# A hybrid block on one core: the interleaved part planned by a model of the engines, with TensorE tied to the plan

## The chip, the cores and the metric

One NeuronCore of one Trainium2 chip runs the whole kernel. The metric is the device time of one execution, in microseconds (us). The kernel before takes 1144.53 us, the median of 3 runs (1142.67 to 1146.72).

## The reference

A transformer block in fp32 for one sequence of 512 positions with 1024 channels. Three mixers of width 512 with 8 heads of 64 read one input projection: softmax attention with a forget gate ("fox"), a gated linear recurrence in chunks of 64 ("hgrn") and a delta-rule recurrence ("rwkv"). Their outputs go through a projection each, are gated and summed, and a convolutional feed-forward part follows.

```python
mod = silu(c) @ w_ada + b_ada                       # shifts, scales and gates, 6 x 1024
h = rms_norm(x) * norm1_g * (1 + sc1) + sh1
fox_p, hgrn_p, rwkv_p, gate_p = split(h @ w_in)     # 1024 -> 1544 + 2048 + 1792 + 3072
y_fox = fox_attention(...)      # rms norm of q and k per head, softmax per 128 queries
y_hgrn = hgrn2_branch(...)      # chunked recurrence, rms norm per head, gate
y_rwkv = rwkv7_branch(...)      # low-rank decay and rate, k normed per head, recurrence, group norm
merged = sum(sigmoid(g_i) * (y_i @ w_branch[i]) for i in range(3))
x = x + gt1 * (merged @ w_out)
h = rms_norm(x) * norm2_g * (1 + sc2) + sh2
u = causal_dwconv(h @ w_up, conv_w, conv_b)         # 5632 channels, 3 taps
x = x + gt2 * ((u_a * silu(u_b)) @ w_down)
```

## The kernel before

Every large product is made of three products of operands that are rounded to the fp32r type and their remainders (`mm3`: high times high, high times low, low times high), with 128x128 weights and 512 moving columns. A weight block comes by SP's queue (`raw`), ScalarE makes its high part (`whi`), VectorE or GpSimd the low one (`wlo`). These are called big products here; they write `mm` tiles in PSUM. All other products are plain fp32, write `br` tiles, and many use a part of the array only: 64x64 (chunks of the recurrences), 128x64, 64x128, 128x32 or 32x32.

The program has a start (modulation, first norm, first projection columns), an interleaved part, and an end (`w_out`, second norm, `w_up`, `w_down`). The interleaved part is the one that changes. It consists of Python generators, the streams: `rwkv_b`, `rwkv_a`, `hgrn` and `fox` for four pairs of heads each (`gi` from 0 to 3), `prep`, `ada_stream` (the later modulation columns, on VectorE), and `big`, which walks the list of projection, gate and merge jobs. `run` (L111) asks them in turn to emit their next piece of code. A stream gives back a latency by hand (`yield 2.0`), and is asked again when a clock `clk` has passed it; `clk` is a count of TensorE's time by rough prices in `mm` (L81) and `transpose` (L91). The first stream in the list whose time has come is taken, so the big products fill what the others leave. `need` (L97) makes a stream wait for what another has posted with a latency.

What `run` emits is then put in order once more by the framework's scheduler, engine by engine, which may draw a ready instruction ahead of an earlier one, TensorE's included. After that each engine executes its own order.

`head_sums` (L447) sums squares over the 64 channels of a head: four products on quarters of the array (a 128x32 weight, 128 moving columns), a VectorE copy `hs` (L457), and a transpose by TensorE. Callers are `rwkv_a` (`ksq`), `hgrn` (`pr`), `fox` (two tiles, `qsq`) and `ada_stream` (`adac`): 16 calls with 20 tiles. In `rwkv_a` the low-rank products of `a` and the decay use a 128-row high part and a 64-row low part of the weight (`w2h`, `w2l`).

Chains that the prediction speaks of, with their lines: softmax of `fox` (logits, masked maximum L708, `nmx` L711, exponential L717, 1/sum L722, scaling of `L` L723, transposes by L93, `PT`); norms of heads (`rn` or `qkr`, power on GpSimd, `rnx` L439, transposes); the state chain of `rwkv_b` (six steps of two 64x64 products and one VectorE step, `ST`, L1031) and its group norm (`gsum`, `gxc` L1051, `gvar`, `gxc` L1060, transposes); the inverse in `rwkv_a` (15 VectorE steps on `lt` and `X`, a write to DRAM `d` and a read back as `Xc`, then 32x32 products on `XZ`).

```python
            for q in range(4):
                mm(ps[32 * q:32 * q + 32, i * P:(i + 1) * P], ones[:, 0:32] if sums else K("hind32"), sq[:, q * P:(q + 1) * P])
        t = T2("hs")
        v.tensor_copy(t[:, :n], ps[:, :n])
        yield 0.6
        ps = PSB()
        for i in range(len(sqs)):
            transpose(ps[:, i * P:(i + 1) * P], t[:, i * P:(i + 1) * P], ident)
```

Of the kernel before, what the change touches and what calls it, by code (L numbers as in the profile page):

```python
# [22 lines left out]
              ("hind32", 32), ("half16", 2), ("nhalf32", 2), ("id64", 64), ("sel8", 8), ("i16", 256), ("causal", 512)]  # L23
# [17 lines left out]

@with_exitstack
def block_kernel(ctx: ExitStack, tc: tile.TileContext, I, out, dbg=None, upto=99):
    nc = tc.nc
    sync, v, s, g, pe = nc.sync, nc.vector, nc.scalar, nc.gpsimd, nc.tensor
    P = 128
# [17 lines left out]
    LAT = (0.9, 1.65)  # L64
# [15 lines left out]
    clk = [0.0]  # L80

    def mm(o, lhsT, rhs, start=True, stop=True):
        n = rhs.free_size() if hasattr(rhs, "free_size") else math.prod(rhs.shape[1:])
        if rhs.dtype == F32R:
            clk[0] += n / 2400
        else:
            half = (0.5 if lhsT.shape[0] <= 64 else 1.0) * (0.25 if math.prod(lhsT.shape[1:]) <= 32 else 1.0)
            clk[0] += half * max(0.17, n / 600)
        return pe.matmul(o, lhsT=lhsT, rhs=rhs, start=start, stop=stop)  # L89

    def transpose(o, i, idn):  # L91
        clk[0] += 0.11 if i.shape[0] > 64 else 0.07
        pe.transpose(o, i, idn)  # L93
# [3 lines left out]
    def need(*keys):  # L97
        for k in keys:
            while k not in avail:
                yield None  # L100
        t = max(avail[k][0] for k in keys) - clk[0]
        if t > 0:
            yield t
        return [avail[k][1] for k in keys]

    def post(key, val, lat=0.0):
        avail[key] = (clk[0] + lat, val)

    def run(streams):

        live = [[gen, 0.0, False] for gen in streams]  # L111
        while live:
            done = False
            for st in live:
                if st[1] > clk[0] + 1e-9:
                    continue
                c0, n0 = clk[0], len(avail)
                try:
                    lat = next(st[0])
                except StopIteration:  # L120
                    live.remove(st)
                    done = True
                    break
                if lat is None and c0 == clk[0] and n0 == len(avail):
                    continue
                lat = lat or 0.0
                st[1] = clk[0] + (lat * LAT[0] + LAT[1] if lat else 0.0)
                done = True
                break
            if not done:  # L130
                later = [st[1] for st in live if st[1] > clk[0] + 1e-9]
                assert later, "streams wait for each other"
                clk[0] = min(later)

    def PSM():
        return psm.tile([P, 512], F32, tag="mm", name=nm("mm"))

    def PSB():
        return psb.tile([P, 512], F32, tag="br", name=nm("br"))
# [186 lines left out]
    def split(raw, shape, leng):  # L326
        hi = wp.tile(list(shape), F32R, tag="whi", bufs=WB[1], name=nm("whi"))
        lo = wp.tile(list(shape), F32R, tag="wlo", bufs=WB[2], name=nm("wlo"))
# [5 lines left out]
    def load(src, r0, nr, c0, ncol):  # L334
        nld[0] += 1
        sh = [P, nr // P, ncol]
        raw = wp.tile(sh, F32, tag="raw", bufs=WB[0], name=nm("raw"))
# [111 lines left out]
    def head_sums(sqs, sums=None):  # L449

        n = len(sqs) * P
        ps = PSB()
        for i, sq in enumerate(sqs):
            for q in range(4):
                mm(ps[32 * q:32 * q + 32, i * P:(i + 1) * P], ones[:, 0:32] if sums else K("hind32"), sq[:, q * P:(q + 1) * P])
        t = T2("hs")
        v.tensor_copy(t[:, :n], ps[:, :n])  # L457
        yield 0.6
        ps = PSB()
        for i in range(len(sqs)):  # L460
# [962 lines left out]
```

## Time and profile before

| | |
|---|---|
| median of 3 runs | 1144.53 us (1142.67 to 1146.72) |
| profiled execution | 1147.7 us, its span 1145.9 us |
| TensorE (PE) busy | 1081.7 us, 94% of the span |
| VectorE (DVE) | 679.2 us, 59% |
| ScalarE (ACT) | 522.9 us, 46% |
| GpSimd (POOL) | 280.0 us, 24% |
| interleaved part | 54.5 to 719.7 us; from 613.4 us on it has big products alone |

The span is the time from the first instruction to the last in the profiled execution, and the rest of its own time lies around it. PE is TensorE's matrix products, PEld its weight loads, which overlap them. A plain fp32 product stands in the trace as two records, one for each pass; a transpose and an fp32r product as one. Matrix products are pipelined, so the start of one to the start of the next is its price, not its listed duration. The granted clock is 1.0 at 2.4 GHz and 0.5 at 1.2 GHz.

### The profile page before, as it was taken

Reading aid. Unit: us, or ns where it says so; the run is one execution under the profiler, and the core shown is the slowest. Engines: PE = TensorE matmul, PEld = TensorE weight load, DVE = VectorE, ACT = ScalarE, POOL = GpSimd, SP = SyncE. Lnnn points to the kernel's source line nnn. Section 1 sums busy time; section 2 is a strip of 40 time slices with the busy share of each in tenths; the row PEclk is TensorE's granted clock in tenths of the full one; section 3 lists DMA queues with packets and bytes.
Section 4 is the critical chain, followed back from the end, with each engine's and each line's share of the span. In section 5 each row is a group of like instructions: output and inputs, shape, how many; then the busy total and the mean of one; then the engine's idle time right before and its main releaser. Section 6 shows DMA issues by size and latency. Waiting matters only on the chain. (4 is left out here: it accounts for less than half of the span.)

```text
span 1145.9 us, 19809 instructions
## 1 busy us (share of the span) xinstructions
PE 1081.7 (94%) x7617; PEld 863.8 (75%) x7617; DVE 679.2 (59%) x1369; ACT 522.9 (46%) x965; POOL 280.0 (24%) x274
## 2 busy tenths in 40 slices
PE   4988999799999999979999999899999999999998
PEld 2566776587777777767878887678888888888886
DVE  1567665858578685784745636536666666661114
ACT  2575464255656656367434335224444444442220
POOL 4015321513334331431021613332111101101100
PEclk8999998889999999989999999899999999999999
DMA  9732233132322440334343565201333333333232
GB/s 315 206 83 71 72 101 89 37 105 72 87 95 50 125 107 20 93 89 135 85 129 102 159 201 179 85 1 56 98 99 93 101 98 96 94 100 100 93 101 83
DMA packets 175476, 117.63 MB, mean 103 GB/s; under 512 B 25360, under 2 KB 151350, under 8 KB 175382
## 3 DMA queue, kind: packets, MB, share of 16 engines
q1 hardware_dynamic: 173696, 116.22, 34.9%
q8 instruction: 60, 0.98, 0.4%
q10 hardware_dynamic: 1238, 0.12, 0.1%
q14 instruction: 34, 0.28, 0.1%
q0 software_dynamic: 448, 0.03, 0.0%
HBM read 112.57 MB, written 3.77 MB: 102 GB/s over the span
## 5 line engine op out<-in xcount | busy, mean ns | idle before, releaser
L330 ACT ACTIVATE whi<-raw 128x512 fp32r<-128x512 f32 x282 | 176.5, 629 | 355.0 <-PE mm L89 226.7
L331 DVE TENSOR_TENSOR wlo<-raw,whi 128x512 fp32r<-128x512 f32 x212 | 150.9, 714 | 156.1 <-ACT whi L330 152.7
L331 POOL TENSOR_TENSOR wlo<-raw,whi 128x512 fp32r<-128x512 f32 x70 | 97.8, 1397 | 495.3 <-ACT whi L330 475.4
L89 PE MATMUL mm<-hhi,whi 128*128 128x512 f32 x504 | 205.5, 408 | 2.6 <-ACT gt L1091 2.3
L89 PE MATMUL mm<-hhi,wlo 128*128 128x512 f32 x504 | 200.2, 397 | 0.0
L89 PE MATMUL mm<-hlo,whi 128*128 128x512 f32 x504 | 200.2, 397 | 0.0
L89 PE MATMUL mm<-h2hlo,whi 128*128 128x512 f32 (+1 forms) x376 | 141.5, 377 | 1.2 <-POOL h2hlo L1273 1.2
L89 PE MATMUL mm<-h2hhi,whi 128*128 128x512 f32 (+1 forms) x376 | 141.3, 376 | 0.0
L89 PE MATMUL mm<-h2hhi,wlo 128*128 128x512 f32 (+1 forms) x376 | 141.2, 376 | 0.0
L89 PEld LDWEIGHTS mm<-hhi,whi 128*128 128x128 f32 x504 | 95.9, 190 | 25.2 <-ACT gt L1091 2.7
L89 PEld LDWEIGHTS mm<-hhi,wlo 128*128 128x128 f32 x504 | 96.0, 190 | 20.7 <-issue 0.2
L89 PEld LDWEIGHTS mm<-hlo,whi 128*128 128x128 f32 x504 | 96.2, 191 | 18.4 <-issue 0.6
L89 PEld LDWEIGHTS mm<-h2hlo,whi 128*128 128x128 f32 x376 | 70.7, 188 | 14.9 <-POOL h2hlo L1273 2.0
L89 PEld LDWEIGHTS mm<-h2hhi,whi 128*128 128x128 f32 x376 | 70.7, 188 | 12.9
L89 PEld LDWEIGHTS mm<-h2hhi,wlo 128*128 128x128 f32 x376 | 70.7, 188 | 12.6
L1331 DVE SCALAR_TENSOR_TENSOR u<-mm,cw,u 128x511 f32<-128x511 f32 x44 | 32.9, 747 | 54.7 <-ACT u L1330 54.7
L1162 DVE SCALAR_TENSOR_TENSOR adac<-ada,cs,adac 128x512 f32<-128x512 f32 x56 | 46.0, 822 | 0.7
L89 PE MATMUL br<-wlo,ahi 128*128 128x512 f32 x110 | 42.8, 389 | 0.0
L89 PE MATMUL br<-whi,ahi 128*128 128x512 f32 x110 | 42.8, 389 | 0.0
L89 PE MATMUL br<-whi,alo 128*128 128x512 f32 x110 | 42.8, 389 | 0.0
L89 PE MATMUL mm<-yhi,whi 128*128 128x512 f32 x96 | 38.3, 399 | 0.8 <-DVE gt L1142 0.7
L89 PE MATMUL mm<-ylo,whi 128*128 128x512 f32 x96 | 37.5, 391 | 0.0
(387 smaller groups left out, 1947.5 us busy)
## 6 DMA issues: line engine op xcount, KB each, us to landing
raw<-in_w_in_dram SPq DMA_DIRECT2D x126, 256.0 KB, 3.1
ada<-in_w_ada_dram SPq DMA_DIRECT2D x96, 256.0 KB, 4.9
raw<-in_w_up_dram SPq DMA_DIRECT2D x88, 256.0 KB, 3.0
raw<-in_w_down_dram SPq DMA_DIRECT2D x44, 256.0 KB, 2.6
raw<-in_w_branch_dram SPq DMA_DIRECT2D x24, 256.0 KB, 2.7
wo<-in_w_out_dram SPq DMA_DIRECT2D x16, 256.0 KB, 4.8
x<-in_x_dram SPq DMA_DIRECT2D x8, 256.0 KB, 4.8
mg<-in_x_dram SPq DMA_DIRECT2D x8, 256.0 KB
```

Of the source, the lines that this page charges most:

```text
L89: return pe.matmul(o, lhsT=lhsT, rhs=rhs, start=start, stop=stop)
L330: s.activation(hi, raw, AF.Copy)
L331: (g if leng == "g" else v).tensor_tensor(out=lo, in0=raw, in1=hi.bitcast(F32), op=ALU.subtract)
L1162: v.scalar_tensor_tensor(out=acc, in0=raws[k], scalar=cs[:, k:k + 1], in1=acc, op0=ALU.mult, op1=ALU.add)
L1331: v.scalar_tensor_tensor(out=u[:, 1:], in0=ps[:, :511], scalar=cw[:, 1, jj:jj + 1], in1=u[:, 1:], op0=ALU.mult, op1=ALU.add)
```

## The change

The planner's clock is replaced by a class `Plan` that follows, for each tile, when it is ready and when it was last used; for each engine of VectorE, ScalarE and GpSimd, a list of busy intervals in which a new instruction takes the first gap; SP's queue and the transfers; TensorE with its array mode; and the buffers of the pools. Wrappers (`Planned`) around the engines feed it with each instruction that the code emits. A stream gives back a kind in place of a latency: "f" (free, any time it is ready), "s" (small, on a part of the array) or "b" (a big product, ready when its weight is). `run` takes a ready free stream first, holds small ones back for up to 3 us while big products are ready and the whole array is in use, and gives them all in a row then. Every product and transpose of the interleaved part is tied behind the one emitted before it, so that the scheduler leaves TensorE's order as planned; the other engines' orders are still the scheduler's. `head_sums` takes the squares as 128x128 weights and two columns (or one) as the moving operand, without a copy and a transpose. The low part of the low-rank weights is filled with zeros to 128 rows, so that its products use the whole array. In `rwkv_a` and `ada_stream` a split and the products that read it become two steps.

```diff
+SEM, DRAIN, CHANGE, ENTER = 0.08, 0.2, 0.11, 0.1
+START, HOLD, SLACK = 47.0, 3.0, 0.1
...
+    def other(self, engine, op, outs, ins):
+        n = outs[0].free_size()
...
+        if engine == "ACT":
+            took = 0.2 + 0.85e-3 * n + (0.19 if len(outs) > 1 else 0.0)
+        elif engine == "POOL":
+            took = 0.3 + 2.2e-3 * n if n > 16 else 0.2 + 0.18 * n
+        else:
+            one = len([a for a in ins if a.free_size() > 8]) < 2 and not psum
+            took = 0.17 + (0.6e-3 if one else 1.15e-3) * n + (0.08 if psum else 0.0)
+        end = self.place(engine, max(self.when((*outs, *ins)), self.slot.get(outs[0].tensor.name, 0.0)) + SEM, took)
...
+    def transfer(self, o, i):
...
+        self.sp = max(self.sp, self.when((o, i)), self.slot.get(o.tensor.name, 0.0)) + 0.1
+        self.dma = max(self.sp, self.dma) + 4 * n / 250e3
+        self.done([o], [i], self.dma + 2.0)
...
+    def in_order(emit):
+
+        if pe_last[0] is None or not strict[0]:
+            r = emit()
+        else:
+            with tc.issue_after(pe_last[0]):
+                r = emit()
+        pe_last[0] = r.ins
+        return r
...
+            small = [st for st in ready if st["kind"] == "s"]
+            free = [st for st in ready if st["kind"] == "f" and not st["big"]]
+            big = [st for st in ready if st["big"]]
+            if plan.whole() and big and small and t - left < HOLD and t - min(st["at"] for st in small) < HOLD:
+                small = []
+            pick = free or small or big
...
-    def head_sums(sqs, sums=None):
-
-        n = len(sqs) * P
-        ps = PSB()
+    def head_sums(sqs, w):
+
+        ps = PSB()
+        n = w.free_size()
         for i, sq in enumerate(sqs):
             for q in range(4):
-                mm(ps[32 * q:32 * q + 32, i * P:(i + 1) * P], ones[:, 0:32] if sums else K("hind32"), sq[:, q * P:(q + 1) * P])
-        t = T2("hs")
-        v.tensor_copy(t[:, :n], ps[:, :n])
-        yield 0.6
...
+                o = (i * 4 + q) * n
+                mm(ps[:, o:o + n], sq[:, q * P:(q + 1) * P], w)
...
-            mm(ps, w2s[i][1][:, gs], L1[i][0:64, :], False, True)
+            mm(ps, w2s[i][1][:, gs], L1[i], False, True)
...
-        yield 1.0
+        yield "f"
+        parts = split2(rk)
+        yield "f"
         psk = PSB()
-        for i, part in enumerate(split2(rk)):
+        for i, part in enumerate(parts):
             mm(psk, bones, part, i == 0, i == 1)
...
             yield from cur[0][1](cur[1])
-            yield 0.0
+            yield "b"
```

What the change does to the engines' orders is shown at three places. The first is TensorE at the second block of 128 queries of the last pair of heads in `fox` (`qk` are the operands of the logits, `L` the softmax tiles that the transposes `br<-con,L` read, `PT` their transposes). Before, from the first block's `PT` on:

```order
L89 MATMUL br_6143<-PT_6108,fv_5975 64x128
L89 MATMUL br_6147<-qk_1231_5809,qk_1229_5807 128x256
L89 MATMUL br_6147<-qk_1235_5813,qk_1233_5811 128x256
L89 MATMUL br_6143<-PT_6112,fv_5975 64x128
L89 MATMUL br_6155<-qk_1232_5810,qk_1230_5808 128x256
L89 MATMUL br_6155<-qk_1236_5814,qk_1234_5812 128x256
L89 MATMUL mm_6128<-hlo,whi_6066 128x512
L89 MATMUL mm_6128<-hhi,wlo_6067 128x512
L89 MATMUL mm_6128<-hhi,whi_6066 128x512
```

In the changed program, the same block:

```order
L221 MATMUL br_6077<-PT_6068,fv_5998 64x128
L221 MATMUL br_6077<-PT_6072,fv_5998 64x128
L221 MATMUL br_6123<-qk_1209_5683,qk_1207_5681 128x256
L221 MATMUL br_6123<-qk_1213_5687,qk_1211_5685 128x256
L221 MATMUL br_6131<-qk_1210_5684,qk_1208_5682 128x256
L221 MATMUL br_6131<-qk_1214_5688,qk_1212_5686 128x256
L225 MATMUL br_6149<-con,L_6126 128x128 x2
L225 MATMUL br_6154<-con,L_6134 128x128 x2
L221 MATMUL br_6159<-PT_6152,fv_5998 64x128
```

Before, big products follow the logits (36 rows, most of them big products, to the first transpose of `L`); in the changed program the transposes follow at once.

The second is VectorE in the group norm of the last pair in `rwkv_b` (`gsum` and `gvar` are sums per head, `adac` is the work of `ada_stream`). Before, from the first sum to the last scaling:

```order
L1048 TENSOR_REDUCE gsum_7017<-ot_6986 128x8
L1049 TENSOR_SCALAR gsum_7017<-gsum_7017 128x8
L331 TENSOR_TENSOR wlo_7080<-raw_7077,whi_7079 128x512
L331 TENSOR_TENSOR wlo_7086<-raw_7083,whi_7085 128x512
L1051 TENSOR_TENSOR gxc_7020<-ot_6986,gsum_7017 128x512
L1160 TENSOR_SCALAR adac_7004<-ada_6988,cs_202 128x512
L1162 SCALAR_TENSOR_TENSOR adac_7004<-ada_6990,cs_202,adac_7004 128x512
L1057 TENSOR_REDUCE gvar_7070<-gsq_7056 128x8
L1162 SCALAR_TENSOR_TENSOR adac_7004<-ada_6992,cs_202,adac_7004 128x512
L434 TENSOR_SCALAR gvar_7070<-gvar_7070 128x8
L331 TENSOR_TENSOR wlo_7121<-raw_7118,whi_7120 128x512
L1060 TENSOR_TENSOR gxc_7020<-gxc_7020,gvar_7070 128x512
```

In the changed program (where L163 is the wrapper's line, which all instructions of the wrapped engines have):

```order
L163 TENSOR_REDUCE gsum_6784<-ot_6779 128x8
L163 TENSOR_SCALAR gsum_6784<-gsum_6784 128x8
L163 TENSOR_TENSOR gxc_6787<-ot_6779,gsum_6784 128x512
L163 TENSOR_TENSOR mg_6792<-mm_6741,gt_6318 128x512
L163 TENSOR_REDUCE gvar_6809<-gsq_6804 128x8
L163 TENSOR_SCALAR gvar_6809<-gvar_6809 128x8
L163 TENSOR_TENSOR gxc_6787<-gxc_6787,gvar_6809 128x512
```

The steps of the chain now stand next to each other but for one step of the merge; `wlo` and `adac` stand elsewhere.

The third is SP's queue at the inverse of the first pair in `rwkv_a` (`d` is the DRAM buffer, `raw` are weight blocks). Before, the last rows up to the read of `Xc` (its write, `d_358_1623<-XZ_941`, stands 13 rows above that read, with four more `raw` rows and the rows of `qk` between):

```order
L670 DMA qk_325_1404<-ncum 3x512
L338 DMA raw_1651<-in_w_in_dram 128x4x128
L338 DMA raw_1736<-in_w_in_dram 128x4x128
L338 DMA raw_1742<-in_w_in_dram 128x4x128
L338 DMA raw_1881<-in_w_in_dram 128x4x128
L940 DMA Xc_1624<-d_358_1623 128x8x16 x2
```

In the changed program:

```order
L163 DMA raw_1458<-in_w_in_dram 128x4x128
L163 DMA raw_1464<-in_w_in_dram 128x4x128
L163 DMA d_293_1309<-XZ_1005 64x256 x2
L163 DMA Xc_1310<-d_293_1309 128x8x16 x2
L163 DMA raw_1635<-in_w_in_dram 128x4x128
```

The read follows its write directly now, and the weight loads that stood between come after both.

## Rows read from the trace of the kernel before

**Rows 1.** The page, busy time, share of the span and instructions.

```profile
PE 1081.7 (94%) x7617; PEld 863.8 (75%) x7617; DVE 679.2 (59%) x1369; ACT 522.9 (46%) x965; POOL 280.0 (24%) x274
```

**Rows 2.** The table by stretches, two of four.

```profile
core 0: us, PE busy (x) PEld busy (x) DVE busy (x) ACT busy (x) POOL busy (x), PEclk, DMA share, GB/s
...
54.50:613.40 558.90, 523.36 (x5066) 413.90 (x5059) 385.09 (x911) 307.45 (x593) 167.93 (x162) 0.97 0.32 88
...
719.70:1145.90 426.20, 413.21 (x1884) 341.99 (x1884) 214.74 (x328) 151.45 (x258) 64.53 (x57) 0.99 0.29 87
```

**Rows 3.** TensorE's waits, 54.5 to 613.4 us: total us, times, longest us.

```profile
PE br L93 <- DVE L L723: 5.8, 3, 4.8
PE br L89 <- DVE ST L1031: 5.4, 5, 1.4
PE br L93 <- DVE rnx L439: 5.2, 3, 2.0
PE br L89 <- DVE slo L467: 3.3, 3, 2.2
PE br L89 <- POOL pr L493: 3.0, 1, 3.0
PE br L89 <- DVE XZ L965: 2.4, 1, 2.4
```

**Rows 4.** TensorE's timeline around one head sum: start us, us, instruction, idle before.

```profile
70.77 0.39 PE L89 MATMUL mm<-hhi,whi 128*128 128x512 f32 x1
71.09 0.43 PE L89 MATMUL br<-ksq,con 128*32 128x128 f32 x8
71.44 0.50 PE L89 MATMUL mm<-hlo,whi 128*128 128x512 f32 x1
71.78 0.39 PE L89 MATMUL mm<-hhi,wlo 128*128 128x512 f32 x1
...
72.71 0.27 PE L93 MATMUL br<-con,hs 128*128 128x128 f32 x1
72.74 0.48 PE L89 MATMUL mm<-hhi,whi 128*128 128x512 f32 x1
73.05 0.40 PE L89 MATMUL mm<-hlo,whi 128*128 128x512 f32 x1
```

**Rows 5.** The same view at 15.95 us: four products with one moving column.

```profile
15.95 1.05 PE L89 MATMUL br<-sel,adap 128*128 128x1 f32 x8 [0.80 <-ACT adap L269]
```

**Rows 6.** The same view: first of four low-rank products, and what follows the fourth.

```profile
64.64 0.47 PE L89 MATMUL br<-lst,w2h 128*128 128x512 f32 x1 [0.69 <-DVE lst L800]
...
66.33 0.50 PE L89 MATMUL mm<-hhi,wlo 128*128 128x512 f32 x1
```

**Rows 7.** The same view: the longest wait, and big products soon after.

```profile
224.05 0.87 PE L93 MATMUL br<-con,L 128*128 128x128 f32 x3 [4.82 <-DVE L L723]
...
226.28 0.63 PE L89 MATMUL mm<-hhi,whi 128*128 128x512 f32 x1
226.71 0.63 PE L89 MATMUL mm<-hlo,whi 128*128 128x512 f32 x1
```

**Rows 8.** Sum over the six stretches of the interleaved part at clock 0.5.

```profile
sum 37.50, PE 36.08 PEld 30.12 DVE 22.02 ACT 12.10 POOL 6.37; mean PE 6.01 PEld 5.02 DVE 3.67 ACT 2.02 POOL 1.06
```

**Rows 9.** VectorE's timeline in the last group norm, the row ahead of `gxc`.

```profile
602.55 0.69 DVE L331 TENSOR_TENSOR wlo<-raw,whi 128x512 fp32r<-128x512 f32 x1 [2.08 <-ACT whi L330]
```

**Rows 10.** Groups by line, 54.5 to 720 us: busy us, mean ns, idle before.

```profile
L717 ACT ACT_TABLE_LOAD x13 | 16.7, 1283 | 3.2 <-DVE nmx L711 1.5 <-DVE rn L836 1.5
L717 ACT ACTIVATE L<-L,nmx 128x256 f32<-128x256 f32 x8 | 4.0, 506 | 0.5 <-DVE nmx L711 0.5
L723 DVE TENSOR_SCALAR L<-L,ri 128x256 f32<-128x256 f32 x8 | 3.4, 422 | 0.1
```

**Rows 11.** DMA issues, the read of `lt`: count, KB, us to landing.

```profile
lt<-d SPq DMA_DIRECT2D x4, 64.0 KB, 4.1
```

More of the change, by code (lines that the diff above doesn't have):

```diff
@@ new lines, with __init__, __getattr__, call @@
+class Planned:
+    def __init__(self, engine, name, plan):
+        self.engine, self.name, self.plan = engine, name, plan
+    def __getattr__(self, op):
+        f = getattr(self.engine, op)
+        def call(*args, **named):
+            aps = [a for a in args if hasattr(a, "tensor")]
+            outs = [named[k] for k in ("out", "accum_out") if named.get(k) is not None]
+            if "out" not in named:
+                outs, aps = [aps[0], *outs], aps[1:]
+            ins = aps + [a for k, a in named.items() if k not in ("out", "accum_out") and hasattr(a, "tensor")]
+            if op == "dma_start":
+                self.plan.transfer(outs[0], ins[0])
+            else:
+                self.plan.other(self.name, op, outs, ins)
+            return f(*args, **named)
+        return call
@@ L100, in need, with post @@
                 yield None
-        t = max(avail[k][0] for k in keys) - clk[0]
-        if t > 0:
-            yield t
+        yield (kind, max(avail[k][0] for k in keys))
         return [avail[k][1] for k in keys]
-    def post(key, val, lat=0.0):
-        avail[key] = (clk[0] + lat, val)
+    def post(key, val):
+        avail[key] = (plan.seg, val)
     def run(streams):
-        live = [[gen, 0.0, False] for gen in streams]
+        strict[0] = True
+        plan.begin(START)
+        live = [dict(gen=gen, at=plan.pe, kind="f", n=-1, big=i == len(streams) - 1) for i, gen in enumerate(streams)]
+        left = plan.pe
@@ L130, in run @@
-            if not done:
-                later = [st[1] for st in live if st[1] > clk[0] + 1e-9]
-                assert later, "streams wait for each other"
-                clk[0] = min(later)
+            t = plan.pe
+            ready = [st for st in live if st["n"] != len(avail) and st["at"] <= t + SLACK]
+            small = [st for st in ready if st["kind"] == "s"]
+            free = [st for st in ready if st["kind"] == "f" and not st["big"]]
+            big = [st for st in ready if st["big"]]
@@ new lines, in run @@
+            if plan.whole() and big and small and t - left < HOLD and t - min(st["at"] for st in small) < HOLD:
+                small = []
+            pick = free or small or big
+            if not pick:
+                later = [st for st in live if st["n"] != len(avail)]
+                assert later, "streams wait for each other"
+                plan.pe = max(plan.pe, min(st["at"] for st in later))
+                continue
+            st = pick[0]
+            was = plan.whole()
+            plan.seg, p0, n0 = 0.0, plan.pe, len(avail)
@@ new lines, in run @@
+            try:
+                y = next(st["gen"])
+            except StopIteration:
+                live.remove(st)
+                continue
+            if plan.whole() and not was:
+                left = plan.pe
+            st["n"] = -1
+            if y is None:
+                st["n"] = n0
+            elif isinstance(y, tuple):
+                st["kind"], st["at"] = y
+            elif isinstance(y, float):
+                st["kind"], st["at"] = "f", plan.pe + y
+            elif y == "b":
+                st["kind"], st["at"] = "b", plan.wready
+            else:
+                st["kind"], st["at"] = y, plan.seg
@@ L135, in PSM @@
+        import os
+        if os.environ.get("PLAN"):
+            print("PLAN end", plan.pe, "idle", plan.idle, "changes", plan.changes)
     def PSM():
-        return psm.tile([P, 512], F32, tag="mm", name=nm("mm"))
+        return plan.alloc("mm", 3, psm.tile([P, 512], F32, tag="mm", name=nm("mm")))
     def PSB():
-        return psb.tile([P, 512], F32, tag="br", name=nm("br"))
+        return plan.alloc("br", 5, psb.tile([P, 512], F32, tag="br", name=nm("br")))
     def dump(name, ap_sb, ap_dram):
@@ L326, in split @@
     def split(raw, shape, leng):
-        hi = wp.tile(list(shape), F32R, tag="whi", bufs=WB[1], name=nm("whi"))
-        lo = wp.tile(list(shape), F32R, tag="wlo", bufs=WB[2], name=nm("wlo"))
+        hi = plan.alloc("whi", WB[1], wp.tile(list(shape), F32R, tag="whi", bufs=WB[1], name=nm("whi")))
+        lo = plan.alloc("wlo", WB[2], wp.tile(list(shape), F32R, tag="wlo", bufs=WB[2], name=nm("wlo")))
         with tc.issue_after(last["hi"]), tc.issue_after(last["mod"]):
@@ L1164, in ada_stream @@
             if 6 <= j < 10:
-                pss = yield from head_sums([acc], "ones32")
+                pss = head_sums([acc], ones[:, 0:1])
                 v.tensor_tensor(out=modc[:, 4 * j:4 * j + 4], in0=pss[:, 0, :, 0], in1=C("b_ada", 4 * j, 4), op=ALU.add)
@@ L1191, in big @@
             cur, nxt = nxt, pick()
+            w = cur[1]
+            plan.wready = plan.when(w[0]) if isinstance(w, list) else 0.0
+            yield "b"
+            plan.wready = 0.0
             yield from cur[0][1](cur[1])
-            yield 0.0
+            yield "b"
     def proj_rest(i, n, j):
```

271 lines of the change are left out of this document (161 added, 110 removed).

## Prediction

> **What bounds the kernel now.** I read the page first: TensorE is busy 94% of the span, the other engines 59% or less [rows 1]. So the time is TensorE's instructions, plus the stretches in which it waits, plus those in which it runs at a lower clock. The table by stretches then tells where the slack lies: from 54.5 to 613.4 us, the interleaved part as long as small work is mixed into it, TensorE is busy 523.4 of 558.9 us, so it waits 35.5 us, at a mean clock of 0.97 [rows 2]. All of the change lies there; the code behind it keeps its order of products but for 13 rows. The list of waits says for what TensorE waits: no single cause, but softmax tiles (`L`), the state chain (`ST`), spread norms (`rnx`), halves of splits (`slo`) and so on, the six longest sums making 25.1 us [rows 3]. They are waits on short chains through VectorE, ScalarE or GpSimd whose reader stood too early in TensorE's order. The clock comes on top: six stretches, 37.5 us together, were granted 0.5, that is the 1.2 GHz level instead of 2.4, and TensorE was busy for 36.08 us of them [rows 8]. In one of them the big products come every 0.43 us instead of 0.23, and it began inside a wait of 4.82 us [rows 7].
>
> **The change, part by part.** The sum is made against the profiled execution, 1147.7 us (its span is 1145.9), which is 3.2 us above the median of the runs.
>
> *Head sums.* Of 20 tiles (12 calls with one, four with two) each cost four products on quarters of the array, one VectorE copy and one transpose. The four products take 0.35 us from their start to the next start; the product ahead of them takes 0.32 instead of 0.23, the one behind 0.34; the later transpose with the product behind it takes 0.34 instead of 0.23: some 0.66 us together [rows 4]. Now it is four products of a whole 128x128 weight with two moving columns. The nearest row is a sum with one column: eight passes (four products) in 1.05 us, of which the last pass's tail is some 0.15, so 0.9 [rows 5]. That is +0.24 us a tile; in a call with two tiles I allow +0.7, since leaving and entering the array is paid once there. 12 x 0.24 + 4 x 0.7 = +5.7 us, taken as +6. Its bounds are +6.4, and 0 if TensorE would have waited in these places anyway. What it buys is a shorter chain: no copy and no second turn on TensorE before the sum can be read.
>
> The trace thus speaks against this edit as far as TensorE's own time goes. The Trainium skill, "TensorEngine Tiling (Array Packing)", section "When to Use Tiling", gives the same as a rule: with few moving columns one should swap the operands and tile the columns, which is the form that is given up here. By the rule alone the edit is a loss of its whole price; by the trace it is that price less the waits on this chain. The same page, "Key Properties", says that changing the tiling mode drains TensorE, and the 0.09 and 0.11 us around the group agree with that.
>
> *Low rank.* Four products take 1.69 us, 0.42 each, since every second one changes to half the array [rows 6]; as whole products at 0.23 they take 0.91. Four times -0.78 is -3.1 us (0 if a wait takes its place). The two memsets that fill the padded halves are hidden by GpSimd's idle time, long before the tiles are read. Without that cover they would delay the first reader once, by an estimated 2 us at most: a GpSimd step on a whole tile, `pr`, was waited for 3.0 us in all [rows 3].
>
> *Changes of array mode.* In the listed order TensorE leaves the whole array 90 times before and 76 times now; without head sums and low rank it is 77 and 76. The new rule that holds small work together therefore saves nothing that the two edits do not, and I cost it at 0.
>
> *Waits that go.* The order decides. Of the 24 readers of the state chain at least 16 stood under 2.8 us of TensorE work behind the step before; now 22 stand 3.4 us (15 big products) or more behind it: -4.5 of 5.4 us. The shortest way from a head sum to its `rnx` grows from 1.9 to 4.9 us: -3.5 of 5.2. Both splits now have a step of their own between the split and its products: -3 of 3.3. The wait for `pr` stood at the start of a hgrn block, and the planner now places it by GpSimd's time: -2.5 of 3.0. `XZ` has 4.1 us or more ahead of each of its readers in the inverse (2.2 before): -2 of 2.4. Of `L`, 4.8 of the 5.8 were one wait; VectorE's work between the first and last step on an `L` tile was up to 14.1 us and is now 7.6 at most, by the rows' durations: -4. All the small ones together -3. Sum -22.5 us.
>
> On the engines that TensorE waits for, order helps the same way. In the last norm chain a `wlo` stood in front of `gxc` on VectorE and waited 2.08 us for a weight [rows 9]; that piece of the queue now holds the chain's own steps and one step of the merge. On SP's queue the read of `Xc` stood behind eight weight loads, now right behind its write.
>
> *Waits that come.* For the last pair of heads the second softmax block now has nothing between its logits and their transposes. The nearest rows are 0.51 us of exponential and 0.42 of scaling for one head, and two heads follow each other, with a first and last step not counted; 2 to 3.5 us [rows 10], taken as +3.5. An earlier such block has 2.1 us of cover: +1. The four `gxc` chains have 6.1 to 10.5 us of products ahead, where their steps alone need some 6.5 without any queue: +2.5. One `VM` reader 2.4 us behind its products: +2.5. A weight load held up behind a `d` write on SP: +2. Sum +11.5; bounds 5 (plan right nearly everywhere) and 40 (see the third rival).
>
> *Clock.* If no stretch fell to 1.2 GHz, the 36.08 us would take half, -18 us. The longest waits of `L`, `pr`, `XZ` and `slo` (4.8, 3.0, 2.4, 2.2) each stand within 5 us before the start of a slow stretch, and go; I take half: -9. Bounds -18 and, if new waits bring new dips, +5.
>
> Sum: +6 - 3.1 - 22.5 + 11.5 - 9 = -17.1, so 1130.6 for a profiled execution and 1127.4 against the median; forecast **1127 us**.
>
> **Rivals.** A difference of 0.3%, 3.4 us, is about what a measurement of this kernel can tell from none.
>
> (1) *The plan holds nearly everywhere.* 30 of the 35.5 us of waits and 14 of the clock's 18 go: 1144.5 + 3 - 30 - 14 = 1103 to 1112. For: the queues of VectorE and SP were shortened with the chains. Against: the order still has the four thin places above.
>
> (2) *The waits only move.* TensorE already executed one fixed order; a new one with the same VectorE load, 385 us in the stretch [rows 2], may wait elsewhere for as long. Then +6 - 3 stays: 1141 to 1148. Against: in the counts above all but a few readers moved away from their writers, few moved closer. It is also how it would look if the model's order did not carry over to the other engines, whose order the scheduler still picks.
>
> (3) *The plan is early wherever its prices lack something, and tied TensorE pays each time.* The planner prices ScalarE by elements and knows no table load; the trace has 1.283 us for each, 13 of them ahead of the softmax exponential alone [rows 10], and 34 stand in the new program. It prices a landing at 2.0 us, the trace has 4.1 for `lt` [rows 11]. Before, the latencies written by hand left 15 to 19 us of products ahead of each `gxc` reader; the plan leaves 6 to 10.5, and a tied TensorE draws no later product ahead. If 28 loads of 1.28 us (36 us) and four chains with two late landings (17 us) reach TensorE in full, and take a few clock dips with them, the waits are some 55 us instead of 35.5: 1144.5 + 3 + 20 = 1167. It decides from the point where more than half of these reach TensorE: 26 us on top of the rest of the waits cancels the gain. For it: single softmax blocks with under 4 us of cover. Against: most `L` readers have 5 to 12 us of cover, which holds a load.
>
> **How the numbers follow.** Forecast 0.50 (1115 to 1138), rival (1) 0.20, rival (2) 0.12, rival (3) 0.18. Faster: 0.50 + 0.20 = 0.70; same 0.12; slower 0.18. The 8-in-10 range leaves out half of rival (1) and half of rival (3): 1107 to 1152.
>
> **What would show it.** Right: waits of TensorE between 54 and about 590 us of 20 to 28 us instead of 35.5; no `ST`, `slo` or `pr` among the longest, `L` with one wait of 2 us or more near the last softmax blocks; half-clock time under 25 us; the head sums' products 0.22 us apart; low-rank products 0.23 apart. Wrong: a list of waits as long as before with other names (rival 2); waits on `L` or `XZ` whose writer stood behind a table load or a landing (rival 3); a tail behind the last branch product that is not the 426 us of before.

## The result and the profile after

The changed kernel takes 1189.71 us, the median of 4 runs (1189.01 to 1190.89), against 1145.18 us for the kernel before on the same chip: a ratio of 1.0389, 95% interval 1.0356 to 1.0421. It is slower by some 44.5 us, where 17 us less was forecast, and it lies outside the range of 1107 to 1152.

The page of the changed kernel, the line that answers to [rows 1]:

```profile
PE 1103.2 (93%) x7597; PEld 888.8 (75%) x7597; DVE 669.5 (56%) x1353; ACT 522.2 (44%) x963; POOL 278.2 (23%) x276
```

The table by stretches, cut where the same pieces of the program begin (columns as in [rows 2]; the second stretch ends with the last small product of the head chains, the third with the last branch product; in [rows 2] the second one ends at 613.4 us, ahead of the last transposes and their products, which take another 1.3 us):

```profile
54.50:623.50 569.00, 513.82 (x4910) 414.04 (x4909) 377.19 (x901) 296.57 (x572) 159.49 (x158) 0.93 0.31 86
623.50:761.60 138.10, 137.38 (x604) 112.87 (x602) 57.92 (x73) 52.55 (x92) 42.16 (x29) 1.00 0.45 129
761.60:1189.10 427.50, 413.56 (x1885) 342.34 (x1884) 214.79 (x328) 151.44 (x258) 64.51 (x57) 0.99 0.29 87
```

The tail takes 427.5 us, 426.2 before [rows 2], so all but 1.3 us of the loss lies in the interleaved part. There TensorE waits 569.0 - 513.8 = 55.2 us beside small work, 35.5 before, and the mean clock falls from 0.97 to 0.93. Small work is over at 623.5 us, 10 us later than before, and 138 us of big products still stand behind it, 106 before. The planned order leaves them there, tied or not: without the tie (experiment 1) as many stand behind the last small product, 603 in 138 us.

The longest rows of the list of TensorE's waits from 54.5 to 761.6 us (columns as in [rows 3]):

```profile
PE br L221 <- POOL pr L163: 14.3, 3, 5.9
PE br L225 <- DVE L L163: 8.4, 3, 7.9
PE br L221 <- DVE slo L163: 6.5, 3, 5.1
PE br L225 <- DVE rnx L163: 5.9, 3, 4.2
PE br L221 <- ACT ksq L163: 5.0, 3, 1.9
PE br L221 <- ACT fp L163: 3.8, 1, 3.8
PE br L221 <- ACT shi L163: 3.7, 3, 1.8
PE br L225 <- DVE on L163: 3.2, 2, 1.9
PE br L221 <- ACT qsq L163: 2.8, 2, 2.3
PE mm L221 <- DVE gt L163: 0.6, 1, 0.6
PE br L221 <- DVE ST L163: 0.5, 1, 0.5
```

Two of the old names are nearly gone (`ST` from 5.4 to 0.5, `XZ` from 2.4 to nothing). `pr`, which the forecast had struck out, is now the longest, and `ksq`, `fp`, `shi`, `on` and `qsq` are new or grown. The same table by stretches over the eleven stretches that were granted 0.5 inside the part, its first, its last and the sum (to be read beside [rows 8]; `...` marks the rows left out):

```profile
60.70:67.50 6.80, 5.67 (x11) 3.21 (x12) 4.70 (x9) 4.36 (x8) 0.00 (x0) 0.50 0.42 117
...
548.80:559.00 10.20, 5.06 (x80) 3.62 (x80) 5.54 (x19) 3.88 (x10) 2.76 (x2) 0.50 0.00 0
sum 74.80, PE 57.00 PEld 43.66 DVE 52.75 ACT 24.76 POOL 24.43; mean PE 5.18 PEld 3.97 DVE 4.80 ACT 2.25 POOL 2.22
```

Half clock lasts 74.8 us, 37.5 before, and TensorE is busy for 57.0 of it, 36.1 before: at half speed that costs 28.5 us instead of 18.

To compare kernels the same way throughout, the table below cuts the profiled execution of each from its first projection product (on `fwh`) to its first `w_out` product. "Waits" is the time between products in which TensorE runs none, "clock" half of the busy time in stretches granted 0.5, and "work" the rest. Each row is one execution; those of the kernel before spread from 1137.2 to 1150.3 us in experiments 1 to 4, so differences of a few us between rows mean little.

| kernel | part, us | waits | clock | work |
|---|---|---|---|---|
| before | 689.5 | 37.1 | 18.0 | 634.4 |
| the change | 729.9 | 57.2 | 29.1 | 643.6 |
| change, no tie | 689.6 | 25.2 | 13.7 | 650.7 |
| change, old head sums | 715.4 | 59.8 | 19.3 | 636.2 |
| change, no tie, old head sums | 679.8 | 26.0 | 11.5 | 642.3 |
| change, two ties | 698.4 | 30.4 | 17.1 | 650.9 |
| before, tied | 714.1 | 59.3 | 20.8 | 633.9 |
| before, new head sums | 694.4 | 24.8 | 21.4 | 648.2 |
| change, window of 8 | 723.5 | 48.1 | 31.1 | 644.3 |
| change, window of 24 | 712.6 | 45.6 | 23.0 | 644.1 |
| change, margin 2.5 us | 756.9 | 68.7 | 45.7 | 642.6 |
| change, table loads priced | 730.0 | 51.7 | 36.5 | 641.8 |
| before, low rank | 678.6 | 37.3 | 7.9 | 633.4 |
| before, low rank and split steps | 677.3 | 26.4 | 15.9 | 634.9 |

The 40.4 us of the part are thus 20.1 of waits, 11.1 of clock and 9.2 of work.

### The profile page after: what moved, and what is told of

It reads as the page before. It is cut to its first block, busy times and chain, and to the rows that moved or that the text cites. A ratio compares the mean times of both kernels' runs of the same rounds, so it can differ in the third digit from the quotient of the medians.

```text
span 1189.1 us, 19765 instructions
## 1 busy us (share of the span) xinstructions
PE 1103.2 (93%) x7597; PEld 888.8 (75%) x7597; DVE 669.5 (56%) x1353; ACT 522.2 (44%) x963; POOL 278.2 (23%) x276
## 5 line engine op out<-in xcount | busy, mean ns | idle before, releaser
L163 ACT ACTIVATE whi<-raw 128x512 fp32r<-128x512 f32 x282 | 177.2, 630 | 357.0 <-PE mm L221 254.3
L163 DVE TENSOR_TENSOR wlo<-raw,whi 128x512 fp32r<-128x512 f32 x212 | 150.7, 712 | 197.5 <-ACT whi L163 196.7
L163 POOL TENSOR_TENSOR wlo<-raw,whi 128x512 fp32r<-128x512 f32 x70 | 92.4, 1320 | 527.4 <-ACT whi L163 520.3
L221 PE MATMUL mm<-hhi,whi 128*128 128x512 f32 x504 | 210.7, 418 | 0.0
L163 DVE SCALAR_TENSOR_TENSOR u<-mm,cw,u 128x511 f32<-128x511 f32 x88 | 65.8, 748 | 56.8 <-ACT u L163 55.3
L163 DVE SCALAR_TENSOR_TENSOR adac<-ada,cs,adac 128x512 f32<-128x512 f32 x56 | 47.9, 856 | 0.4
```

The lines of the kernel that those rows point to most:

```text
L163: return f(*args, **named)
L221: return in_order(lambda: pe.matmul(o, lhsT=lhsT, rhs=rhs, start=start, stop=stop))
```

## The experiments

Each ratio is to the kernel before in the same set of runs on the same chip, with its 95% interval. A change of 0.01 is 11.4 us.

**1. Without the tie.**

```diff
-        strict[0] = True
+        strict[0] = False
```

> The changed kernel with the tie of TensorE's products taken away; plan, head sums and low rank stay. Changed kernel: 1189.7 us, 57.2 us of TensorE's waits from the first product of the part to the first w_out product, 74.8 us at half clock. Theory TIE (the plan is early and a tied TensorE must stand and wait where an untied one draws a ready product ahead): waits under 40 us, 1145 to 1162 us. Rival QUEUE-ONLY (the lateness sits in the queues of VectorE and ScalarE, and the order of TensorE that the scheduler picks is as blind to it): 1180 us or more, waits over 50 us.

Measured: 1147.47 us, ratio 1.0038 (1.0008 to 1.0068). Of the 3.9% all but 0.4% go with this one word. Waits fall to 25.2 us, clock to 13.7, work rises by 7.1: the untied order leaves the whole array 98 times instead of 76, which would make 0.32 us for each if nothing else adds to it. The theory of the tie holds.

**2. The new head sums alone, on the kernel before.**

```diff
-                mm(ps[32 * q:32 * q + 32, i * P:(i + 1) * P], ones[:, 0:32] if sums else K("hind32"), sq[:, q * P:(q + 1) * P])
+                mm(ps[:, o:o + n], sq[:, q * P:(q + 1) * P], w)
```

(with the copy and the transposes left out, as in the change)

> The kernel before with the new head sums alone (squares as 128x128 weights, two moving columns or one, no copy, no second turn). Prediction's term: +6 us, so 1151 us; its lower bound 0 (1145) if TensorE would have waited there anyway. Rival (the shorter chain moves waits as well, its sign unknown): outside 1143 to 1154. In no theory more than 15 of the 44.5 us.

Measured: ratio 1.0095 (1.0056 to 1.0134), so +10.9 us, nearly twice the term, and outside 1143 to 1154 as the rival had it. The shorter chain did move waits: in the profile of this kernel the part waits 12.3 us less than before, but its work is 13.8 us more and its clock costs 3.4 more (table above).

**3. Table loads in the plan's prices.**

```diff
+            new = [TABLES[a] for a in args if isinstance(a, type(AF.Exp)) and a in TABLES]
+            if op == "activation" and new and new[0] != self.plan.table:
+                self.plan.table, self.plan.load = new[0], 1.28
```

> The changed kernel with 1.28 us in the plan's price of a ScalarE instruction whose table differs from the one before it in the order of emission. Theory TABLES (rival 3 as predicted: the loads that the plan does not know make it early): waits fall from 57 to 35 us or less, half-clock time by a third, 1150 to 1168 us. Theory QUEUE (the plan gives an instruction the first gap of its engine, the engine executes in the scheduler's order, behind weight splits and other chains): the wait for L shrinks (7.9 us to about 6), the waits for pr, slo, ksq stay, 1180 to 1192 us.

Measured: 1189.39 us, ratio 1.0421 (1.0379 to 1.0463); waits of the part 51.7 us instead of 57.2, half clock 78.5 us. The first three rows of this kernel's list, 54 to 790 us:

```profile
PE br L233 <- DVE rnx L171: 11.0, 4, 4.0
PE br L229 <- DVE XZ L171: 7.0, 2, 5.4
PE br L229 <- POOL pr L171: 6.4, 3, 3.9
```

The waits on `pr` and `L` do shrink, from 14.3 to 6.4 and from 8.4 to 1.8, but `rnx` and `XZ`, 5.9 and nothing in the changed kernel, take their place, and the clock takes the rest. A plan that knows the loads wins no time, though single late writers do stand behind a load, as the rows further below show.

**4. A margin on every step.**

```diff
-                st["kind"], st["at"] = y, plan.seg
+                st["kind"], st["at"] = y, plan.seg + 2.5
...
-        avail[key] = (plan.seg, val)
+        avail[key] = (plan.seg + 2.5, val)
```

> The changed kernel with 2.5 us added to the time at which a step or a posted result counts as ready. Theory QUEUE: steps come 2.5 us later each, lateness that grew to 5 to 10 us at pr, slo, L is only partly covered: waits 25 to 38 us, half clock 35 to 55 us, 1150 to 1168 us. Theory TABLES: the loads (1.28 us, rarely two on a chain) are covered altogether, waits under 25 us, 1135 to 1150 us. If neither (the lateness follows the order on the other engines whatever the margin): within 6 us of 1189.7.

Measured: 1216.76 us, ratio 1.0653 (1.0620 to 1.0686): worse by 27 us, which no theory had foreseen. The last small product comes at 702.7 us instead of 623.2, and the waits are 68.7 us, among them `rnx` (11.7), `L` (8.4) and `gxc` (8.0). Big products did not run out: 365 still stand behind the last small one. An even margin lengthens every chain, and the longest waits of the changed kernel (5 to 8 us) are two to three times as long as it; why the waits grew with it is not shown.

**5. and 6. The old head sums in the planned order, untied and tied.**

```diff
-                mm(ps[:, o:o + n], sq[:, q * P:(q + 1) * P], w)
...
+                mm(ps[32 * q:32 * q + 32, i * P:(i + 1) * P], w, sq[:, q * P:(q + 1) * P])
+        t = T2("hs")
+        v.tensor_copy(t[:, :n], ps[:, :n])
+        yield "f"
```

> The changed kernel without the tie and with the old head sums (quarters of the array, copy, transpose) in the planned order: plan, low rank and split steps are left of the change. Theory PRICE (whole-array head sums cost about 11 us wherever they stand, as the kernel before with them alone showed, 1.0095): 11 us under the untied kernel, ratio to before 0.989 to 0.997. Rival COVER (the longer chain of copy and transpose brings waits that eat the price): within 3 us of the untied kernel's ratio of 1.0038.

> The changed kernel, tied as it is, with the old head sums. PRICE: 11 us under it, ratio 1.026 to 1.033 to before (the change: 1.0389). COVER: a tied TensorE waits for the longer chain, so the ratio stays at 1.036 or rises over 1.042.

Measured: untied 0.9961 (0.9937 to 0.9986), tied 1.0316 (1.0294 to 1.0339). So the new sums cost 0.73% with the tie and 0.77% without it, 8.4 and 8.8 us, each good to some 4 us. It is a price and not a wait: in the table the work differs by 7.4 and 8.4 us and the waits by 2.6 and 0.8, the other way; the clock of these executions differs by 9.8 and 2.2 as well. And the tie costs 3.55% with the old sums, 3.51% with the new: within the intervals the two effects just add.

**7. The tie on the kernel before**, its own planner kept: the same wrapper `in_order` around its products.

```diff
-        return pe.matmul(o, lhsT=lhsT, rhs=rhs, start=start, stop=stop)
+        return in_order(lambda: pe.matmul(o, lhsT=lhsT, rhs=rhs, start=start, stop=stop))
```

> The kernel before with every product and transpose of the interleaved part tied behind the one emitted before it, its own planner and latencies kept. Theory TIE-ITSELF (any emission order costs much if TensorE may not pass a late product): 15 us or more over before, waits over 50 us instead of 37. Rival PLAN-EARLY (it is the new plan that puts readers too near, the old latencies written by hand are safe): within 5 us of before.

Measured: 1176.02 us, ratio 1.0305 (1.0280 to 1.0331). The order that the old planner wrote is as bad a one to be tied to as the new. TensorE's waits in this kernel, 54.5 to 745 us, the first three of the list:

```profile
PE br L100 <- DVE slo L479: 17.5, 6, 10.8
PE br L104 <- DVE rnx L451: 9.9, 4, 4.8
PE br L100 <- DVE ST L1043: 8.6, 4, 4.5
```

Other names than with the new plan, the same sum (59.3 against 57.2 us).

**8. Two ties**, one for big products and one for small.

```diff
+        big = o.tensor.name.startswith("mm")
...
-            with tc.issue_after(pe_last[0]):
+            with tc.issue_after(pe_last[big]):
```

> The changed kernel with two ties in place of one: big products among themselves, small ones among themselves; the scheduler may slide one row against the other. If the loss is that big products stand behind a late small one: waits under 40 us, 1145 to 1165 us. If small ones block each other as well (a late one of one stream holds those of the others): 1165 to 1185 us.

Measured: 1156.83 us, ratio 1.0135 (1.0109 to 1.0161). Most of the loss is that big and small products stand behind each other, big ones behind a late small one above all, though the edit frees small ones of late big ones as well; some 1% is that small ones hold up each other or that big products keep their order.

**9. and 10. A window.** Each product is tied behind the 24th, or the 8th, before it.

```diff
-            with tc.issue_after(pe_last[0]):
+            with tc.issue_after(pe_last[-24]):
```

> The changed kernel with each product tied behind the 24th before it in place of the last one, so that a ready product may pass up to 23 others (24 big products are 5.4 us). Theory LOCAL (single late readers; the waits are 1 to 8 us long): most of the 42 us come back, waits 25 to 38 us, 1150 to 1165 us. Rival GLOBAL (the planned order is out of step with the other engines for long stretches, so a short look ahead ends in the same waits): waits over 45 us, 1172 us or more.

> The same with the 8th before it (8 big products are 1.8 us). LOCAL: between the window of 24 and the full tie, as the waits of 1.8 us and less go whole and the others lose 1.8 us each: waits 38 to 50 us, 1165 to 1180 us. GLOBAL: 1182 us or more.

Measured: 1.0237 (1.0211 to 1.0263) for 24 and 1.0334 (1.0310 to 1.0359) for 8. Between the two theories: with 24 the time, 1171.48 us, just misses the bound of the global one and the waits, 45.6 us, just fit it; with 8 the time, 1183.27 us, is the global one's and the waits, 48.1 us, are the local one's. The window of 8 gives back 6 of the 44.5 us, that of 24 gives back 17, which suggests that a good part of the readers is out of place by more than 24 products. In the untied order 511 of the part's 3945 products and transposes stand over ten places ahead of where the plan had them, the furthest 129.

**11. and 12. Half of the weights' low parts on GpSimd**, in the changed kernel and in the untied one with old head sums.

```diff
-    LO_POOL = 4
+    LO_POOL = 2
```

> The changed kernel, tied, with every second weight block's low part on GpSimd instead of every fourth, so that some 50 us of weight splits leave VectorE's queue. Theory QUEUE (readers are late because their writers stand behind weight splits and other chains in VectorE's queue): waits of TensorE fall from 57 to 35 to 48 us, 1160 to 1182 us. Rival: the plan, which prices that load too, only writes another order, as early as this one: within 5 us of 1189.7, waits over 52 us.

> The untied kernel with old head sums (ratio 0.9961) and every second low part on GpSimd. QUEUE: VectorE's chains come sooner, 3 to 6 us less, ratio 0.990 to 0.994. Rival: with an untied TensorE what is left of waits (26 us) is not VectorE's queue, or the slower GpSimd split makes weights late: 0.995 to 1.004.

Measured: tied 1.0326 (1.0298 to 1.0355), at the far end of what a relieved queue should give, with waits of 52.6 us where 35 to 48 were expected: the time is the theory's, some 7 us less, the waits are the rival's. Untied 1.0063 (1.0040 to 1.0085), 1% slower than without. How much work stands in VectorE's queue is at most a small part of the loss.

**13. Tables priced in the untied kernel with old head sums** (the edit of experiment 3).

> The untied kernel with old head sums and the table loads priced in the plan. Theory TABLES for an untied TensorE: a plan that knows them is worth 2 to 5 us, ratio 0.991 to 0.994. If the scheduler makes up for what the plan lacks: within 0.3% of 0.9961.

Measured: 0.9976 (0.9960 to 0.9992), the same as without within the intervals. Knowing the tables is worth nothing here.

**14., 15. and 16. The two small parts on the kernel before**, together and each alone.

```diff
-            mm(ps, w2s[i][1][:, gs], L1[i][0:64, :], False, True)
+            mm(ps, w2s[i][1][:, gs], L1[i], False, True)
...
+        parts = split2(rk)
+        yield 1.0
         psk = PSB()
-        for i, part in enumerate(split2(rk)):
+        for i, part in enumerate(parts):
```

(the split in `ada_stream` likewise)

> The kernel before with two small parts of the change alone: low-rank products on the whole array, and a step of its own between a split and its products. Prediction's terms: -3.1 for the low rank, about -3 for waits on slo: 1139 us, ratio 0.993 to 0.997. If this equals the untied kernel with old head sums (0.9961), the new plan's order is worth nothing by itself; if it is 0.999 to 1.003, the plan is worth that kernel's whole gain of about 4 us.

> The kernel before with the low-rank products on the whole array alone. Prediction's term: -3.1 us, ratio 0.9973 (0.995 to 0.999). If it is the larger part of the two: 0.992 to 0.995.

> The kernel before with the step of its own between split and products alone. Prediction's term: -3 us of waits on slo, ratio 0.9974 (0.995 to 0.999). If it is the larger part: 0.992 to 0.995.

Measured: together 1134.42 us, 0.9917 (0.9894 to 0.9941), under the 0.993 to 0.997 of the terms; low rank alone 0.9972 (0.9952 to 0.9991); split steps alone 0.9941 (0.9922 to 0.9960). **The kernel before with these two edits is the fastest of the study**, 9.5 us under before. It is also 0.44% under the untied kernel with old head sums, which has both edits and the new plan as well: by the middle values the new plan's order costs 5 us even untied, though the intervals just overlap.

The loss in parts, by these ratios: low rank and split steps -9.5, the plan's order +5, the new head sums +8.4, the tie +40.6; together 44.5 us. Each part is good to some 3 to 5 us.

## Why the prediction was wrong

**The tie had no term.** The prediction costed head sums, low rank, array modes, waits and clock, and let the tie appear only in the third rival ("a tied TensorE draws no later product ahead"). It was the change: 3.5% by itself with the new plan, whichever head sums stand beside it, and 3.0% with the old one. What it was good for, fewer changes of array mode, it did bring: 7.1 us less of work than without it.

**The step that failed is "Waits that go".** It counted how many microseconds of TensorE's own products stand between a reader and the step before, and took a longer distance for a wait gone. With "Waits that come" it made 11 us less of waits; they came out 20 us longer. Of the waits that it struck out only those for `ST` and `XZ` went; `pr` was to lose 2.5 us and gained 11.3, `slo` was to lose 3 and gained 3.2, `rnx` was to lose 3.5 and gained 0.7. The distance leaves out when the writer's engine gets to its step. The third wait for `pr`, 5.75 us, shows it. TensorE's timeline of the changed kernel, columns as in [rows 4]:

```profile
344.71 1.16 PE L221 MATMUL br<-AR,BK 64*128 64x128 f32 x8
351.62 0.59 PE L221 MATMUL br<-con,pr 128*128 128x2 f32 x2 [5.75 <-POOL pr L163]
```

GpSimd makes `pr` out of `hq` and `kt`. `hq` needs `sg`, a sigmoid by ScalarE; `kt` needs `gate`, whose own sigmoid `sig` ScalarE had finished at 325.1 us. The timelines of ScalarE, VectorE and GpSimd ahead of it, rows cut between the engines:

```profile
344.33 0.63 ACT L163 ACTIVATE whi<-raw 128x512 fp32r<-128x512 f32 x1 [2.83 <-PE mm L221]
344.98 1.28 ACT L163 ACT_TABLE_LOAD   x1
346.28 0.60 ACT L163 ACTIVATE sg<-mm 128x512 f32<-128x512 f32 x1
...
345.10 0.28 DVE L163 SCALAR_TENSOR_TENSOR ST<-br,wc,ST 128x64 f32<-128x64 f32 x1
346.91 0.69 DVE L163 TENSOR_TENSOR hq<-mm,sg 128x512 f32<-128x512 f32 x1 [1.52 <-ACT sg L163]
347.51 0.48 DVE L163 TENSOR_SCALAR adac<-ada,cs 128x512 f32<-128x512 f32 x1
347.90 0.54 DVE L163 TENSOR_SCALAR gate<-sig,omlb,lb 128x512 f32<-128x512 f32 x1
348.36 0.75 DVE L163 SCALAR_TENSOR_TENSOR adac<-ada,cs,adac 128x512 f32<-128x512 f32 x1
349.02 0.43 DVE L163 TENSOR_SCALAR ft<-gate 128x512 f32<-128x512 f32 x1
349.36 0.42 DVE L163 TENSOR_SCALAR kt<-gate 128x512 f32<-128x512 f32 x1
...
349.86 1.71 POOL L163 TENSOR_TENSOR pr<-hq,kt 128x512 f32<-128x512 f32 x1 [3.50 <-DVE kt L163]
```

In these rows each engine keeps to the order of its queue. ScalarE stands idle for 2.83 us with a weight's `whi` at its head, which waits for a big product, and then loads a table for 1.28 us before `sg`. VectorE stands idle 1.52 us because `hq` at its head waits for `sg`, with `gate` behind it; `gate`, `ft` and `kt`, some 1.1 us from start to start, would have fitted there. Instead they and two steps of `adac` come behind `hq`, and `pr` starts 2.3 us after `hq` is through. The plan gives every instruction the first gap of its engine after its operands are ready; the queue has no such gaps. In the untied kernel VectorE's order from `hq` to `kt` is the same, row for row, but TensorE's reader stands later, among big products, and waits for nothing (its timeline, the same piece):

```profile
332.95 0.39 PE L221 MATMUL mm<-hlo,whi 128*128 128x512 f32 x1
333.17 0.95 PE L221 MATMUL br<-con,pr 128*128 128x2 f32 x8
334.05 0.33 PE L221 MATMUL br<-ST,MT 64*64 64x64 f32 x4
```

So the untied scheduler writes a TensorE order that fits the orders it gives to the other engines, and neither of the two tied orders fits them. That the scheduler does so because it settles all engines in one pass is the likely reason, but it is only argued and not shown. Three other reasons were tried one by one: knowing the table loads moves the waits to other names and wins nothing (experiment 3), less work on VectorE wins 7 us (experiment 11), and an even margin costs 27 (experiment 4). None of them is the reason by itself.

Without the tie the part waits 25.2 us, inside the 20 to 28 of the forecast. That does not speak for the planned order: the kernel before with low rank and split steps alone waits 26.4.

**`L` was seen in the right place and mis-sized.** The forecast named the last softmax blocks, where the transposes now follow the logits at once, and gave +3.5 us; the wait is 7.9 (545.92 to 553.83 us). VectorE's timeline between logits and transposes:

```profile
548.06 0.69 DVE L163 TENSOR_TENSOR ylo<-yh,yhi 128x512 fp32r<-128x512 f32 x1 [1.97 <-ACT yhi L163]
549.10 1.34 DVE L163 TENSOR_TENSOR ylo<-yh,yhi 128x512 fp32r<-128x512 f32 x1 [0.34 <-ACT yhi L163]
550.36 0.41 DVE L163 CUSTOM_DVE_ANT_0 L<-br,con 128x256 f32<-128x256 f32 x1
```

And ScalarE's:

```profile
545.62 1.28 ACT L163 ACT_TABLE_LOAD   x1
546.91 0.60 ACT L163 ACTIVATE gt<-mm 128x512 f32<-128x512 f32 x1
547.41 2.17 ACT L163 ACTIVATE yhi<-yh 128x512 fp32r<-128x512 f32 x4
551.29 1.28 ACT L163 ACT_TABLE_LOAD   x1 [1.71 <-DVE nmx L163]
```

The logits end at 545.9 us, but the mask step on `L` begins at 550.4, behind two low parts of branch outputs that wait for ScalarE: 4.4 us of queue that the forecast's sum of the chain's own steps left out. The table loads that the third rival spoke of are there too, two of them: one ahead of `gt`, in front of the `yhi` that VectorE's queue waits for, and one ahead of the exponential. Together they take 2.3 of the 7.9 us at most.

**Head sums** were mis-sized: +6 forecast, with 6.4 as the upper bound, against 8.4, 8.8 and 10.9 measured. The new price was right: 0.88 us in the rows above, 0.9 forecast from [rows 5]. The old one was too high: the forecast took the sum between two big products [rows 4] as the typical case. Beside other small work, as here in the kernel before, the array is changed anyway, and the four products cost 0.36 us and the transpose 0.17 (TensorE's timeline of the kernel before):

```profile
198.13 0.64 PE L89 MATMUL br<-UV,G 128*64 128x64 f32 x16
198.69 0.43 PE L89 MATMUL br<-ksq,con 128*32 128x128 f32 x8
199.05 0.33 PE L93 MATMUL br<-con,hs 128*128 128x128 f32 x1
199.22 0.38 PE L93 MATMUL br<-con,L 128*128 128x128 f32 x2
```

Summed over all 20 tiles, from start to next start and without idle time, the old products take 7.0 us and their transposes 2.4 in the kernel before, the new products 17.6 in experiment 2: 8.2 us more, which is nearly the whole of what experiments 5 and 6 measured. The lower bound, that TensorE would have waited there anyway, did not decide; only in the kernel before did the waits fall by much with the new sums, by 12.3 us, and that kernel lost time all the same. The rule of the Trainium skill that the prediction set against this edit ("TensorEngine Tiling (Array Packing)", "When to Use Tiling": few moving columns, so swap the operands and tile) gave the right sign, and these runs agree with it: the edit costs 8.4 to 10.9 us.

**Clock** was forecast at -9 and came at +10.5, because it hung on waits that did not go. All eleven half-clock stretches of the part began inside a wait of 1.4 us or more or within 2.4 us of its end, though not each such wait was followed by one (1.9 us at 531.6 us was not). Waits alone do not set the sum: tied with the old head sums, the part waits 59.8 us and the clock costs 19.3.

**What held.** Low rank: -3.1 forecast, 0.9972 measured, which is -3.2 (-1.0 to -5.5 by its interval). All its 16 products take 4.4 us from start to next start where they took 6.9, so 2.5 of the 3.1 show in the trace. Its first four products stand 0.23 to 0.30 us apart (TensorE's timeline of the kernel with this edit alone):

```profile
65.40 0.47 PE L89 MATMUL br<-lst,w2h 128*128 128x512 f32 x1 [0.68 <-DVE lst L801]
65.70 0.40 PE L89 MATMUL br<-lst,w2l 128*128 128x512 f32 x1
65.94 0.39 PE L89 MATMUL br<-lst,w2h 128*128 128x512 f32 x1
66.17 0.40 PE L89 MATMUL br<-lst,w2l 128*128 128x512 f32 x1
```

Split steps: the right sign, -3 forecast and -6.8 measured where nothing is tied; there the waits for `slo` fall from 3.3 to 0.7 us, as forecast, and the rest came elsewhere. In the tied kernel TensorE still waits 6.5 us for `slo`. `ST` and `XZ` went as forecast, the tail stayed, and of the new waits those for `gxc`, `VM` and a weight behind a `d` write did not come.

**The rivals.** The third came nearest: it said that a tied TensorE pays for each lateness, and some 55 us of waits, which is what the profile shows (55.2). Its reasons, loads and landings that the plan does not know, are at most a part: loads stand in front of `pr` and `L`, but to price them wins nothing (experiments 3 and 13); landings were not tried. Its time, 1167 us, was 23 too low: it allowed +3 for work and no sum of its own for the clock, where work came at 9.2 and the clock at 11.1. The second, that the waits only move, has the time of the change without the tie (1147.47 us), but not its mechanism: there the waits fell by 11.9 us and the work rose by 16.3.

## What to carry to other kernels

Before tying an engine to a planned order, cost the tie by itself, with the old order too: here it was 3.0% with the old plan and 3.5% with the new. A planner that lets instructions fall into the first gap of an engine describes no engine that executes a queue in order; look in the trace at what stands at the head of each queue in front of a late writer, ScalarE's too, not only at the distance between writer and reader on TensorE. And split a bundle of edits early: two small ones in this one are worth 9.5 us, and would have been given up with the rest.

## What the runs showed of the hardware that was not expected

Waits can cost more than their length, but at no fixed rate. In the changed kernel 20.1 us of added waits came with 11.1 us of clock, TensorE at 1.2 GHz while busy; with the margin 31.6 us of added waits came with 27.7. But the changed kernel with old head sums and the kernel before with the tie wait 22.7 and 22.2 us longer than before, and their clock costs only 1.3 and 2.8 us more. The low-rank kernel waits 37.3 us, as long as before, and is granted 0.5 for 17.5 us instead of 37.5.

GpSimd is a poor place for more weight splits in the untied kernel. A low part takes it 1.33 us, VectorE 0.75; with 141 instead of 70 of them on GpSimd that kernel is 1% slower and waits 38.7 us instead of 26.0. The tied kernel gained 7 us by the same edit.
